# First feed-forward layer of a decoder layer: the high and low halves of the input as one moving operand of 512 columns

## The chip, the cores and the metric

The kernel runs on one core of a Trainium2 chip. The metric is the device time of one execution in microseconds (us); lower is better. The times given for a version are medians of several runs. The profile comes from one execution of its own, taken by the hardware profiler. A core has a tensor engine (PE in the profile; PEld is its loading of weights), a vector engine (DVE), a scalar engine (ACT), GpSimd (POOL), and queues that start DMA transfers (SP's is the one used most here). Tensor results land in PSUM, which has eight banks of 512 four-byte columns in each of 128 partitions; everything else works from SBUF.

## What is computed

One decoder layer on 256 positions of 2048 channels, in float32: a token mixer (three recurrent branches, far the larger part of the code) and then a gated feed-forward layer, each with a residual and a layer norm. The change touches the feed-forward part, cut here to what matters (the bias and the width-3 convolution run along the positions):

```python
def conv_ffn(h, w_up, conv_w, conv_b, w_down):       # h: (1, 256, 2048)
    hcat = causal_dwconv(h @ w_up, conv_w, conv_b)   # w_up: (2048, 2 * 5504)
    gate, up = jnp.split(hcat, 2, axis=-1)
    return (gelu(gate) * up) @ w_down                # w_down: (5504, 2048)
...
h = layer_norm(alpha * x + mix, ln1_g, ln1_b)
h = layer_norm(alpha * h + conv_ffn(h, ...), ln2_g, ln2_b)
```

## The kernel before

All large products are made from a split into two parts: a float32 operand a is rounded to float32r, the format that the matmul takes here (the high half), and the rounding's remainder is kept as a second float32r tensor (the low half). A product is then three matmuls summed in PSUM: high x high, high x low and low x high.

**Weights.** `chunks` (L216 to L243) brings a weight matrix in pieces of two contraction tiles of 128 rows (KC = 2) and up to 512 columns. A DMA on SP's queue fills `wraw` (four buffers), ScalarE casts it to `whi` (L239), VectorE subtracts to get `wlo` (L240); `whi` and `wlo` have three buffers each. These steps have high priority: the program is put in order by a scheduler that simulates the engines, and among instructions that are ready it takes those of high priority first. Each engine then runs its own list strictly in that order.

**The first layer's matmuls.** In `ffn` (L1211), the loop at L1226 goes over the 43 tiles of 128 channels two at a time, so 22 passes ("blocks", 0 to 21; the last has one tile). A block makes the gate columns and the up columns of its tiles: four column tiles of 128, two in the last block. It calls `proj_cm`, which is `cm_units` (L248): for each of the 16 contraction tiles and each column tile j, three matmuls with 128x128 weights as the stationary operand and 256 columns (the positions) of the input as the moving one:

```python
nc.tensor.matmul(a, lhsT=wh, rhs=X.h(kt), ...)   # L256: high weight, high input
nc.tensor.matmul(a, lhsT=wh, rhs=X.l(kt), ...)   # L258: high weight, low input
nc.tensor.matmul(a, lhsT=wl, rhs=X.h(kt), ...)   # L260: low weight, high input
```

Two column tiles share a PSUM bank (`acc`, pool psA, four banks), so a block takes two banks and neighbouring blocks alternate. The other four banks (pool psM: tags `mix` and `seq`, two each) belong to the mixer and to the transposes.

**What follows a block.** For each column tile, `conv` (L382) reads the bank: ScalarE makes the first tap with the bias (L384), VectorE adds two more taps, shifted by one and two positions (L387). Then Gelu on ScalarE (L1235), the product of gate and up on GpSimd (L1236), and the split into the halves of A, the second layer's input: a cast on ScalarE (L296) and a subtraction on VectorE (L297).

**The input X.** `x_pair` (L391) makes two tiles, `xh` and `xl`, of 16 contraction tiles x 256 columns each. `to_cm` (L300) fills them: it transposes the normalised rows into `mix` banks (L309), ScalarE writes the scaled high half (L314), VectorE the same in float32 (L315), and VectorE subtracts for the low half (L317). Block 0 starts while this goes on. At the same time `affine_tm` (L351) scales the rows that the residual needs, on GpSimd (L360), with the vectors of ln1 brought by DMA into the page `b4` (L358). The mixer has an X of its own from the same function.

**The second layer.** `residual_tm` (L363) runs `tm_units` (L271) with the input as the stationary operand and 512 columns of weights as the moving one (L278 to L280), two psA banks at a time, 43 contraction tiles, four times. The tile `gt`, for the ln2 vectors, takes the place of `xh` (L1239); its DMAs are issued at L1243.

Of the kernel before, what the change touches and what calls it, by code (L numbers as in the profile page):

```python
# [9 lines left out]
F32 = mybir.dt.float32  # L10
F32R = mybir.dt.float32r
AF = mybir.ActivationFunctionType
ALU = mybir.AluOpType
# [4 lines left out]
P = 128  # L18
T = 256
D = 2048  # L20
KT = D // P
KC = 2
NB = D // 512
FFN = 5504
# [154 lines left out]
class Layer:  # L179
# [68 lines left out]
    def cm_units(self, W, pieces, cts, X, nkt=KT):  # L248
# [13 lines left out]
            yield True  # L262
        return [acc[j // 2][:m, j % 2] for j, (o, m) in enumerate(cts)], acc

    def block_cm(self, W, c0, X, nct=4, nkt=KT):
        return self.proj_cm(W, [(0, c0, nct * P)], [(P * j, P) for j in range(nct)], X, nkt)

# [121 lines left out]
                                           in1=dst[:, j:], op0=ALU.mult, op1=ALU.add)  # L389

    def x_pair(self):  # L391
        return Pair([self.xp.tile([P, KT, T], F32R, name="xh")], [self.xp.tile([P, KT, T], F32R, name="xl")], KT)


    def prologue(self):
# [815 lines left out]
    def ffn(self, r):  # L1211
        nc, a, cp = self.nc, self.a, self.cp
        X = self.x_pair()
# [9 lines left out]
        where = lambda kt: (kt // 8, kt % 8) if kt < 16 else (2 + (kt - 16) // 4, kt % 4)  # L1223
        A.h = lambda kt: A.hi[where(kt)[0]][:, where(kt)[1]]
        A.l = lambda kt: A.lo[where(kt)[0]][:, where(kt)[1]]
        for c in range(0, FT, 2):  # L1226
            n = min(2, FT - c)
            ps, _ = self.proj_cm(a["ffn_w_up"], [(0, c * P, n * P), (n * P, FFN + c * P, n * P)],
                                 [(P * j, P) for j in range(2 * n)], X)
            t = [self.pg("s%d" % (i + c % 4), [P, 2, T], "fc") for i in range(2)]  # L1230
            for i in range(2):
                for j in range(n):
                    self.conv(ps[i * n + j], t[i][:, j], "fcw", 2 * FT, i * FT + c + j, 3, "fcb", fv)
            u = t[0][:, :n]
            nc.scalar.activation(out=u, in_=u, func=AF.Gelu)  # L1235
            nc.gpsimd.tensor_tensor(out=u, in0=u, in1=t[1][:, :n], op=ALU.mult)  # L1236
            i, k = where(c)
            self.split(A.hi[i][:, k:k + n], A.lo[i][:, k:k + n], u)
        gt = self.xp.tile([P, 4, 2, 512], F32, name="xh")  # L1239

        def load(j):
            for i, nm in enumerate(("ln2_g", "ln2_b")):
# [5 lines left out]
        for tt in range(2):  # L1248
            rstd, nmr, mu = self.moments(st, tt, True)
            for j in (2, 0, 1, 3):  # L1250
                t, g, b = r[j][:, tt], gt[:, j, 0], gt[:, j, 1]
# [4 lines left out]
                else:  # L1256
# [3 lines left out]
                    out=self.out[0, tt * P:(tt + 1) * P, 512 * j:512 * j + 512], in_=t)  # L1260
# [64 lines left out]
```

## Time and profile before

| | |
|---|---|
| median of 3 runs | 2454.65 us (2451.3 to 2455.12) |
| the profiled execution | 2451.87 us |
| its span, first to last instruction | 2450.1 us |
| mean granted tensor clock | 0.984 of full |
| data read, written | 430.19 MB, 14.72 MB |
| the first layer's last matmul starts | about 2202 us |

The span is what the profile's shares refer to; the rest of the execution's time lies around it. The page of a profile gives, per engine, its busy time as a share of the span, then the span in 40 slices, the DMA queues, the chain of work that ended last, and groups of instructions by source line. A group's line reads: source line, engine, operation, output tile, input tiles and shapes, count, then busy time in us and the mean duration of one in ns, then the engine's idle time just before them and what ended it. Timeline lines read: start in us, duration in us, engine, line, operation, and in brackets the idle time before it and who ended that. Matmuls are pipelined: the duration of one is longer than the distance from its start to the next one's start.

### The profile page before, as it was taken

To read this page: it belongs to the slowest core of one execution; us is meant where nothing else is said; L and a number is where in the kernel's file an instruction comes from. 1 tells how busy PE (TensorE), PEld (TensorE's weight loads), DVE (VectorE), ACT (ScalarE), POOL (GpSimd) and SP (SyncE) were. 2 spreads that over 40 slices of the span, in tenths; PEclk is the share of its full clock that TensorE was granted. 3 is DMA by queue.
4 is the path that set the end of the run, shared out by engine and by line. 5 is a ranking of instruction groups with operands and counts; after the bars stand their busy time and mean duration, and the time that the engine had idled before them with its cause. 6 is when DMAs were issued, how large, how long until landed. Compare 5 with 4: busy or idle time off the path is not lost.

```text
span 2450.1 us, 41499 instructions
## 1 busy us (share of the span) xinstructions
PE 2369.3 (97%) x16602; PEld 2131.2 (87%) x16602; DVE 1546.7 (63%) x1856; ACT 1247.3 (51%) x1648; POOL 509.5 (21%) x512
## 2 busy tenths in 40 slices
PE   7999998999999999999999998999999999999997
PEld 7898797798777899998889987787999999998886
DVE  6685575676674566786555666557766666665445
ACT  4554654556464555665434566444555455454333
POOL 0046255264363011423010001301200000000000
PEclk9899999999999999999999999999999999999999
DMA  8445454555565776665766664755655655557664
GB/s 241 144 147 164 140 158 147 154 155 164 148 186 164 213 229 179 183 190 190 263 218 188 174 181 155 238 190 175 189 182 185 185 181 182 186 169 234 194 195 148
DMA packets 283730, 447.66 MB, mean 183 GB/s; under 512 B 25816, under 2 KB 118416, under 8 KB 283152
## 3 DMA queue, kind: packets, MB, share of 16 engines
q1 hardware_dynamic: 280368, 433.99, 58.1%
q10 hardware_dynamic: 2592, 8.91, 0.9%
q8 instruction: 130, 2.13, 0.4%
q0 software_dynamic: 576, 2.10, 0.2%
q14 instruction: 64, 0.52, 0.1%
HBM read 430.19 MB, written 14.72 MB: 182 GB/s over the span
## 4 chain that ended last, share of the span: by engine, by line
PE 83%; POOL 6%; DVE 4%; ACT 3%; DMA 2%; issue 2%; SPq 0%; DVEq 0%; ACTq 0%; POOLq 0%
PE acc L256 13%; PE acc L260 13%; PE acc L258 13%; PE acc L278 13%; PE acc L279 12%; PE acc L280 12%; POOL yi L785 3%; POOL si L783 2%; POOL res L360 1%; DVE wlo L164 1%; PE mix L741 1%; ACT whi L163 1%; DVE wlo L240 1%; PE mix L628 1%; PE mix L1023 1%
## 5 line engine op out<-in xcount | busy, mean ns | idle before, releaser
L240 DVE TENSOR_TENSOR wlo<-wraw,whi 128x1024 fp32r<-128x1024 f32 (+2 forms) x548 | 703.3, 1284 | 519.5 <-ACT whi L239 514.2
L239 ACT CAST whi<-wraw 128x1024 fp32r<-128x1024 f32 (+2 forms) x548 | 569.6, 1041 | 656.5 <-PE acc L280 298.9
L256 PE MATMUL acc<-xh,whi 128*128 128x256 f32 x3104 | 885.1, 286 | 4.9 <-ACT whi L239 2.9
L260 PE MATMUL acc<-xh,wlo 128*128 128x256 f32 x3104 | 881.3, 284 | 5.0 <-DVE wlo L164 4.5
L258 PE MATMUL acc<-xl,whi 128*128 128x256 f32 x3104 | 880.9, 284 | 2.8 <-DVE xl L317 2.8
L256 PEld LDWEIGHTS acc<-xh,whi 128*128 128x128 f32 x3104 | 597.3, 193 | 9.2 <-ACT whi L239 3.5
L260 PEld LDWEIGHTS acc<-xh,wlo 128*128 128x128 f32 x3104 | 596.9, 192 | 7.9 <-DVE wlo L164 5.8
L258 PEld LDWEIGHTS acc<-xl,whi 128*128 128x128 f32 x3104 | 597.7, 193 | 4.8 <-DVE xl L317 3.7
L164 DVE TENSOR_TENSOR wlo<-wraw,whi 128x1024 fp32r<-128x1024 f32 x208 | 278.6, 1351 | 239.1 <-ACT whi L163 238.9
L163 ACT CAST whi<-wraw 128x1024 fp32r<-128x1024 f32 x208 | 216.7, 1049 | 118.3 <-PE acc L280 58.3
L279 PE MATMUL acc<-wlo,xh 128*128 128x512 f32 x640 | 255.5, 399 | 9.9 <-DVE wlo L164 9.8
L278 PE MATMUL acc<-whi,xh 128*128 128x512 f32 x640 | 262.1, 414 | 0.1
L280 PE MATMUL acc<-whi,xl 128*128 128x512 f32 x640 | 253.9, 397 | 0.0
L279 PEld LDWEIGHTS acc<-wlo,xh 128*128 128x128 f32 x640 | 122.9, 192 | 34.5 <-DVE wlo L164 12.0
L278 PEld LDWEIGHTS acc<-whi,xh 128*128 128x128 f32 x640 | 122.4, 191 | 29.5 <-issue 1.2
L280 PEld LDWEIGHTS acc<-whi,xl 128*128 128x128 f32 x640 | 122.9, 192 | 26.3
L279 PE MATMUL acc<-wlo,ah 128*128 128x512 f32 x322 | 125.4, 389 | 0.2 <-DVE wlo L240 0.2
L280 PE MATMUL acc<-whi,al 128*128 128x512 f32 x322 | 125.3, 389 | 0.0
L1236 POOL TENSOR_TENSOR fc<-fc 128x512 f32<-128x512 f32 (+1 forms) x22 | 27.9, 1268 | 453.0 <-DVE fc L387 445.0
L278 PE MATMUL acc<-whi,ah 128*128 128x512 f32 x322 | 111.9, 389 | 0.0
L785 POOL TENSOR_TENSOR yi<-yi,si 128x126 f32<-128x126 f32 (+22 forms) x124 | 84.9, 684 | 9.7
L387 DVE SCALAR_TENSOR_TENSOR fc<-acc,fcols,fc 128x255 f32<-128x255 f32 (+1 forms) x172 | 77.0, 478 | 14.0 <-ACT fc L384 12.5
(357 smaller groups left out, 3025.6 us busy)
## 6 DMA issues: line engine op xcount, KB each, us to landing
wraw<-in_w_in SPq DMA_DIRECT2D x368, 512.0 KB, 3.7
wraw<-in_ffn_w_up SPq DMA_DIRECT2D x336, 256.0 KB, 3.0
wraw<-in_ffn_w_down SPq DMA_DIRECT2D x84, 512.0 KB, 4.4
wraw<-in_proj_rwkv SPq DMA_DIRECT2D x32, 512.0 KB, 4.2
wraw<-in_proj_ssd SPq DMA_DIRECT2D x32, 512.0 KB, 4.5
wraw<-in_proj_mlstm SPq DMA_DIRECT2D x32, 512.0 KB, 4.5
wraw<-in_w_out SPq DMA_DIRECT2D x32, 512.0 KB, 4.2
gdram<-gate ACTq DMA_DIRECT2D x16, 512.0 KB, 3.4
```

Source lines behind the costliest of these rows:

```text
L163: nc.scalar.copy(out=hi, in_=self.raw[i])
L164: nc.vector.tensor_tensor(out=lo, in0=self.raw[i], in1=hi.bitcast(F32), op=ALU.subtract)
L239: nc.scalar.copy(out=hi[:, :n, :width], in_=r)
L240: nc.vector.tensor_tensor(out=lo[:, :n, :width], in0=r, in1=hi[:, :n, :width].bitcast(F32), op=ALU.subtract)
L256: nc.tensor.matmul(a, lhsT=wh[:, o:o + m], rhs=X.h(kt), start=st, stop=False, skip_group_check=True)
L258: nc.tensor.matmul(a, lhsT=wh[:, o:o + m], rhs=X.l(kt), start=False, stop=False, skip_group_check=True)
L260: nc.tensor.matmul(a, lhsT=wl[:, o:o + m], rhs=X.h(kt), start=False, stop=kt == nkt - 1, skip_group_check=True)
L278: nc.tensor.matmul(acc[tt], lhsT=X.h(kt)[:, s], rhs=wh, start=kt == 0, stop=False)
L279: nc.tensor.matmul(acc[tt], lhsT=X.h(kt)[:, s], rhs=wl, start=False, stop=False)
L280: nc.tensor.matmul(acc[tt], lhsT=X.l(kt)[:, s], rhs=wh, start=False, stop=kt == nkt - 1)
L387: nc.vector.scalar_tensor_tensor(out=dst[:, j:], in0=ps[:, :T - j], scalar=v(wname, (width - 1 - j) * nch + ct), in1=dst[:, j:], op0=ALU.m ...
L785: gps.tensor_tensor(out=Yo[:, j + 1:32, :e], in0=Yo[:, j + 1:32, :e], in1=tv, op=ALU.subtract)
```

## The change

The two halves of X become one tile, `xhl`, with the high half first; `X.both` is the whole of it. Every user of `x_pair` gets it, the mixer too; only the first feed-forward layer uses `both`. There a new function, `wide_cm`, takes the place of `proj_cm`:

- For each contraction tile and column tile, the high weight is multiplied with both halves of the input in one matmul, whose moving operand is 2 x 256 columns and whose output is a whole bank: the left half takes high x high, the right half high x low. The low weight's matmul adds to the left half.
- Each column tile so has a bank of its own, four in a block. Even blocks take them from psA, odd blocks from `mix` and `seq`.
- After the last matmul ScalarE copies each bank's right half to a scratch tile `half` in SBUF (page `b4`), and VectorE adds it onto the left half, in PSUM. The convolution then reads the left half as before.
- `gt` takes the place of the joint tile.

```diff
+    def wide_cm(self, W, pieces, n, X, odd, tmp):
+        nc = self.nc
+        acc = [self.bank(t) for t in ("mix", "mix", "seq", "seq")[:n]] if odd else [
+            self.psA.tile([P, 512], F32, name="acc") for _ in range(n)]
+        for kt, wh, wl in self.chunks(W, KT, pieces):
+            for j in range(n):
+                s = slice(P * j, P * j + P)
+                nc.tensor.matmul(acc[j].rearrange("p (a t) -> p a t", a=2), lhsT=wh[:, s], rhs=X.both[:, :, kt],
+                                 start=kt == 0, stop=False, skip_group_check=True)
+                nc.tensor.matmul(acc[j][:, :T], lhsT=wl[:, s], rhs=X.h(kt), start=False,
+                                 stop=kt == KT - 1, skip_group_check=True)
+        for j, a in enumerate(acc):
+            nc.scalar.copy(out=tmp[:, odd, j], in_=a[:, T:])
+        for j, a in enumerate(acc):
+            nc.vector.tensor_tensor(out=a[:, :T], in0=a[:, :T], in1=tmp[:, odd, j], op=ALU.add)
+        return [a[:, :T] for a in acc]
...
     def x_pair(self):
-        return Pair([self.xp.tile([P, KT, T], F32R, name="xh")], [self.xp.tile([P, KT, T], F32R, name="xl")], KT)
+        both = self.xp.tile([P, 2, KT, T], F32R, name="xhl")
+        x = Pair([both[:, 0]], [both[:, 1]], KT)
+        x.both = both
+        return x
...
+        half = self.pg("b4", [P, 2, 4, T], "half")
         for c in range(0, FT, 2):
             n = min(2, FT - c)
-            ps, _ = self.proj_cm(a["ffn_w_up"], [(0, c * P, n * P), (n * P, FFN + c * P, n * P)],
-                                 [(P * j, P) for j in range(2 * n)], X)
+            ps = self.wide_cm(a["ffn_w_up"], [(0, c * P, n * P), (n * P, FFN + c * P, n * P)], 2 * n, X,
+                              c // 2 % 2, half)
...
-        gt = self.xp.tile([P, 4, 2, 512], F32, name="xh")
+        gt = self.xp.tile([P, 2, 4, 2, 512], F32, name="xhl")[:, 0]
```

## The prediction

> **What bounds the kernel now.** I read the page first: total span, busy shares, chain of waits.
>
> ```profile
> span 2450.1 us, 41499 instructions
> PE 2369.3 (97%) x16602; PEld 2131.2 (87%) x16602; DVE 1546.7 (63%) x1856; ACT 1247.3 (51%) x1648; POOL 509.5 (21%) x512
> PE 83%; POOL 6%; DVE 4%; ACT 3%; DMA 2%; issue 2%; SPq 0%; DVEq 0%; ACTq 0%; POOLq 0%
> ```
>
> TensorE carries 83% of the chain that ended last. That is an average, so I next asked for the stage that the change touches, by windows (columns: window, its length, then PE, PEld, DVE, ACT and POOL busy with their counts, granted clock, DMA share, GB/s), and for the PE waits from 1735 us to 2260 us.
>
> ```profile
> 1690.00:1714.00 24.00, 19.22 (x132) 17.75 (x131) 20.80 (x27) 9.65 (x17) 11.26 (x4) 0.86 0.31 78
> 1714.00:1737.00 23.00, 19.80 (x157) 18.80 (x156) 21.59 (x24) 12.16 (x17) 10.29 (x4) 1.00 0.63 190
> 1867.78:1890.82 23.04, 23.04 (x194) 23.04 (x193) 14.43 (x18) 11.48 (x14) 1.29 (x1) 1.00 0.58 177
> PE acc L279 <- DVE wlo L240: 0.2, 1, 0.2
> ```
>
> Two regimes show. From block 1 on, PE never stops: one full block of the loop at L1226 is 23.04 us with PE busy in all of it, the clock granted at 1.00, and in the whole stage the only recorded PE wait is 0.2 us, after its end. VectorE has 23.04 - 14.43 = 8.61 us to spare per block, ScalarE 11.56 us. Block 0 is different: it runs while the normalised input is still being turned round, VectorE is busy 21.59 of 23 us, and PE only 19.80. So a gain in PE's own steps is worth its full size in blocks 1 to 21, and little in block 0.
>
> The third view is what one PE step takes. Busy times overlap (matmuls are pipelined), so I use starts in the timeline, not durations. First ScalarE's first convolution step of three neighbouring blocks:
>
> ```profile
> 1867.78 0.57 ACT L384 ACTIVATE fc<-acc,fcols 128x256 f32<-128x256 f32 x1 [1.24 <-PE acc L260]
> 1890.82 0.56 ACT L384 ACTIVATE fc<-acc,fcols 128x256 f32<-128x256 f32 x1 [1.24 <-PE acc L260]
> 1913.86 0.57 ACT L384 ACTIVATE fc<-acc,fcols 128x256 f32<-128x256 f32 x1 [1.24 <-PE acc L260]
> ```
>
> A block is 16 contraction tiles x 4 column tiles x 3 matmuls = 192 of 256 columns, in 23.04 us: 0.1200 us each. For 512 columns the row is the second feed-forward layer, 322 of each of its three matmuls (columns: ns min/median/max, first and last start):
>
> ```profile
> L279 PE MATMUL acc<-wlo,ah x322: 389/389/496, 2203.2 to 2421.5; 128*128 128x512 f32 x161
> 2299.78 0.39 PE L278 MATMUL acc<-whi,ah 128*128 128x512 f32 x1
> 2301.82 0.39 PE L279 MATMUL acc<-wlo,ah 128*128 128x512 f32 x1
> ```
>
> From the first to the last: 321 x 3 = 963 steps in 218.3 us, 0.2267 us; nine steps from 2299.78 to 2301.82 give 0.2267 too. The 256 extra columns cost 0.2267 - 0.1200 = 0.1067 us, and 256 columns alone would be that again: so each step of 256 carries 0.0133 us that does not grow with columns.
>
> **The change, part by part.**
>
> *Matmuls.* Per contraction tile and column tile, two steps of 256 (L256, L258) become one of 512; the third (L260) stays. 0.3600 us becomes 0.2267 + 0.1200 = 0.3467 us: 0.0133 us less. The weight load between them goes as well; PEld lies beside PE throughout, and whatever it sets is within these start-to-start times. Blocks 1 to 20 hold 64 such units each, block 21 half: 1312 units x 0.0133 = **17.5 us** gained. The trace has no 512-column operand in two runs of 256, nor a 512 step followed by a 256 step. Bounds: at best the narrow step loses its 0.0133 too, because more hides behind the wide one (35 us in all); at worst the two runs cost as two steps (0). I take 17.5, from the 512-column row, the nearest.
>
> One page speaks against a gain of this size. The Trainium skill (TensorE: Matmul & The Clock Gate, "Wait — 56ns, not 53.3ns?") puts the fixed cost of a warm back-to-back matmul at about 2.5 ns beyond its columns. By that, an estimate from that page, 1312 merged pairs would bring 3.3 us. The trace does not agree: its rows give 13.3 ns.
>
> *Evacuation.* Each column tile gets one ScalarE copy of 128x256 from PSUM and one VectorE add of 128x256 that reads and writes PSUM, 86 of each.
>
> ```profile
> L384 ACT ACTIVATE fc<-acc,fcols 128x256 f32<-128x256 f32 x86 | 46.3, 561 | 30.0 <-PE acc L260 27.9 <-DVE fc L387 2.1
> L870 ACT COPY zvo<-seq 64x256 f32<-64x256 f32 x16 | 5.9, 368 | 0.4
> L880 DVE TENSOR_TENSOR zm<-zm,seq 128x256 f32<-128x256 f32 x8 | 3.4, 419 | 5.2 <-PE seq L876 5.2
> L387 DVE SCALAR_TENSOR_TENSOR fc<-acc,fcols,fc 128x255 f32<-128x255 f32 x86 | 39.3, 478 | 12.5 <-ACT fc L384 12.5
> L315 DVE TENSOR_SCALAR tocm<-mix,cst 128x256 f32<-128x256 f32 x16 | 8.4, 539 | 2.4 <-ACT xh L314 2.4
> L297 DVE TENSOR_TENSOR al<-fc,ah 128x512 fp32r<-128x512 f32 x21 | 14.3, 680 | 0.0
> ```
>
> The copy lies between the 64-partition copy's 0.37 us and the 0.56 us of the activation that reads the same bank at the same shape; I take 0.56, the same shape. No VectorE row writes PSUM: 0.42 (a two-input add reading PSUM) to 0.54 us; I take 0.45. A full block adds 4 x 0.56 = 2.2 us to ScalarE and 4 x 0.45 = 1.8 us to VectorE: 13.7 and 16.2 us of the new 22.2 us block. Both fit, so I cost them at nothing in blocks 1 to 20. The cover is the weight pieces cut ahead, three buffers deep:
>
> ```profile
> 1877.02 1.05 ACT L239 CAST whi<-wraw 128x1024 fp32r<-128x1024 f32 x1 [0.38 <-PE acc L258]
> 1878.10 1.23 DVE L240 TENSOR_TENSOR wlo<-wraw,whi 128x1024 fp32r<-128x1024 f32 x1 [0.43 <-ACT whi L239]
> 1879.90 1.05 ACT L239 CAST whi<-wraw 128x1024 fp32r<-128x1024 f32 x1 [1.83 <-PE acc L258]
> ```
>
> A cast starts when PE lets go of the buffer, once per 2.88 us chunk, and its low half is ready at 1879.33, 2.31 us later. The piece is wanted two chunks after the release: today 5.76 - 2.31 = 3.4 us of slack, afterwards two chunks of 8 x 0.3467 = 2.77 us less 2.31, so 3.2 us. Behind a copy or a convolution step that waits stand the casts on ScalarE's queue, and behind an add the subtractions on VectorE's; as long as a cast is held up by less than 3.2 us, PE sees nothing. If that cover goes, the excess is paid at every block end.
>
> *Banks.* A block now takes four banks, even blocks the four of psA, odd blocks the mix and seq pairs. A bank is wanted again one block (22.2 us) after its block ends. VectorE's work at a block end is 4 adds, 8 taps and one split, 4 x 0.45 + 8 x 0.48 + 0.68 = 6.3 us; with 2.77 - 1.23 = 1.54 us free per chunk that takes four chunks, some 11 us. Nothing waits. The second layer takes two of psA, which block 20 held, and here the cover is only the half-length block 21:
>
> ```profile
> 2190.34 0.57 ACT L384 ACTIVATE fc<-acc,fcols 128x256 f32<-128x256 f32 x1 [1.66 <-PE acc L260]
> 2188.71 0.69 DVE L240 TENSOR_TENSOR wlo<-wraw,whi 128x512 fp32r<-128x512 f32 x1 [2.19 <-ACT whi L239]
> 2196.56 0.48 DVE L387 SCALAR_TENSOR_TENSOR fc<-acc,fcols,fc 128x254 f32<-128x254 f32 x1
> 2202.38 0.63 PE L278 MATMUL acc<-whi,ah 128*128 128x512 f32 x2
> ```
>
> Block 20 is emptied in 6.7 us (2190.34 to 2197.04), and block 21 lasts 12.0. Afterwards block 21's half-width chunks take 1.39 us and leave VectorE 1.39 - 0.69 = 0.70 us each: all four banks would take nine of them, 12.5 us, against 11.1 us (32 x 0.3467). The second layer starts with two of the four, which come first, after about half of that. I charge 0.5 us, bounds 0 to 2.
>
> *Block 0 and the joint tile.* A wide matmul needs both halves of a contraction tile, where L256 could start on the high one. The page scratch "half" takes tag b4, which GpSimd's last ln1 scaling holds:
>
> ```profile
> PE acc L258 <- DVE xl L317: 2.8, 3, 1.4
> 1720.68 0.40 PE L256 MATMUL acc<-xh,whi 128*128 128x256 f32 x2
> 1724.10 5.21 POOL L360 TENSOR_TENSOR res<-res,gb 128x1024 f32<-128x1024 f32 x2 [3.94 <-DMA gb<-in_ln_g]
> 1729.33 0.57 ACT L384 ACTIVATE fc<-acc,fcols 128x256 f32<-128x256 f32 x1 [2.82 <-PE acc L260]
> ```
>
> PE already waits for the low half, 2.8 us in three waits; before the longest of them two steps of L256 had gone ahead (1720.68), so what the wide form can lose there is two steps, 0.24 us, each time. b4 comes free at 1729.31, just as block 0 is emptied; one more scaling (half of 5.21 us) of delay would be under the 3.2 us. VectorE is full here, and four adds (1.8 us) come on top. I give block 0 no gain and a loss of 0.5 us, bounds 0 to 2. Elsewhere (the mixer's own X, the ln2 vectors that now wait for the joint tile's release instead of xh's) the same last readers stand within three matmuls, 0.36 us: nothing.
>
> *Sum.* 17.5 - 0.5 - 0.5 = 16.5 us. The profiled execution took 2451.87 us, 1.77 over its span, and lies 2.8 below the median of 2454.65: 2435.4 for it, **2438 us** against the median.
>
> **The rivals.**
>
> *The evacuation stalls PE (slower).* Place: ScalarE's queue at each block end. If the four copies and four convolution steps stand ahead of a cast, with one add between, the cast is late by 8 x 0.56 + 0.45 = 4.9 us, 1.7 us past the slack. At the ends of blocks 0 to 20 that is 21 x 1.7 = 36 us, less 17.5: 18 us slower, 2473 us. It decides from 3.2 us of delay on; at 4.1 us (0.85 past) the gain is just eaten. For it: the new add puts a VectorE turn between two ScalarE steps. Against: today's casts slip in between the convolution steps (high priority at L226), and the hold-up between two of them is 0.95 us (below); and each column tile's own bank frees the steps from each other. Chance 0.11.
>
> ```profile
> 1869.33 1.02 ACT L384 ACTIVATE fc<-acc,fcols 128x256 f32<-128x256 f32 x2
> 1871.30 1.05 ACT L239 CAST whi<-wraw 128x1024 fp32r<-128x1024 f32 x1 [0.95 <-ACT fc L384]
> ```
>
> *The step cost belongs to something that the merge keeps (no gain that can be measured).* If most of the 13.3 ns is what a weight load leaves uncovered, the two loads that remain per unit can show again what the merged step saves: the load for the next wide step has only the narrow step's 0.12 us over it. The price lies between 0 and 17.5 us of gain; I set it at a fifth, 3.5 us, less 1 for the ends: 2452 us. The page named above has a gain of nearly this size. Against: the 512-column rows carry the same 13.3 ns with 0.2267 us over each load. Chance 0.06.
>
> *Two runs cost as two steps.* The wide operand's halves lie 16 KB apart in a partition (16 x 256 elements of 4 bytes); if each run pays its own 0.0133, a unit stays at 0.36 us and the end losses remain: 2455 us. No row of that form speaks for or against. Chance 0.05.
>
> *The narrow step hides its own cost too.* 35 us less 1: 2421 us. Against: nothing shows a 256 step under 0.12 us at full clock. Chance 0.04.
>
> **How the numbers follow.** The forecast has 0.74; its own bounds are 2437 (no end loss) to 2441 us (4 us of it). For 8 in 10 the range starts lower, at 2431, for a narrow step that hides a third of its own cost too (6 us), and reaches up to the rival whose gain can't be measured, 2452; outside lie the slower case, the two runs and the full extra gain, 0.20. A difference of 0.2% is 4.9 us, about what a measurement here can tell from none. Faster by more: 0.74 + 0.04 = 0.78. Within: 0.06 + 0.05 = 0.11. Slower: 0.11.
>
> **What would show each step.** In the profile after, over a block in mid-stage: starts of a wide and the next narrow step 0.2267 and 0.1200 us apart; 1376 steps of 512 columns and as many of 256 instead of 3 x 1376; first convolution or copy steps of neighbouring blocks 22.2 us apart; no PE wait on L239 or L240 between 1735 us and the end of the stage; copies near 0.56 and adds near 0.45 us; the second layer starting some 16 us earlier, its own length unchanged. I am wrong if a unit is not near 0.347 us, if PE waits at block ends add up to more than a few us, or if the second layer's start waits for block 20's banks.

## The result and the profile after

Over four runs of each, the changed kernel takes 2437.14 us (2436.71 to 2440.01) and the kernel before 2454.89 us (2451.3 to 2455.67): a ratio of 0.9933, 95% interval 0.9921 to 0.9945, so 0.7% faster. The forecast was 2438.0 us. The profiled execution of after took 2437.14 us. Its page, answering to the three page lines of before:

```profile
span 2435.3 us, 38930 instructions
PE 2352.3 (97%) x15226; PEld 2054.2 (84%) x15226; DVE 1566.2 (64%) x1942; ACT 1274.4 (52%) x1734; POOL 512.3 (21%) x512
PE 81%; POOL 6%; DVE 5%; DMA 4%; ACT 3%; issue 2%; SPq 0%; DVEq 0%; ACTq 0%; POOLq 0%
```

There are 1376 matmuls fewer (16602 less 15226), one for each merged pair, and 86 instructions more on ScalarE (1734 against 1648) and on VectorE: the copies and the adds. The span is 14.8 us shorter. Where that lies shows in the starts. Two lines of before's PE timeline and groups (in the group: ns min/median/max, first and last start):

```profile
1690.80 0.38 PE L309 MATMUL mix<-cst,res 128*128 128x128 f32 x2
```
```profile
L278 PE MATMUL acc<-whi,ah x322: 387/389/397, 2202.4 to 2421.3; 128*128 128x512 f32 x161
```

And the same two of after:

```profile
1692.20 0.38 PE L328 MATMUL mix<-cst,res 128*128 128x128 f32 x2
```
```profile
L297 PE MATMUL acc<-whi,ah x322: 387/389/398, 2186.7 to 2406.1; 128*128 128x512 f32 x161
```

The first line is where PE turns from the mixer to the feed-forward part, 1.4 us later after the change; the second is the second layer, which starts 15.7 us earlier. So the first layer with its lead-in went from 511.6 us (2202.4 - 1690.8) to 494.5 (2186.7 - 1692.2), 17.1 us less. From the second layer's start to the end of the span it is 247.7 us before and 248.6 after. -17.1 + 1.4 + 0.9 = -14.8, the span's difference. The last two terms lie where the change moved no work, and runs of one kernel differ by more than that (above).

In the stage itself, by windows (window, length, then PE, PEld, DVE, ACT and POOL busy with counts, clock, DMA share, GB/s), first before, then after:

```profile
1800.00:1900.00 100.00, 100.00 (x836) 100.00 (x835) 64.62 (x78) 50.83 (x64) 6.46 (x5) 1.00 0.60 185
```
```profile
1714.00:1737.00 23.00, 19.95 (x111) 16.27 (x110) 22.14 (x25) 12.21 (x20) 10.22 (x4) 1.00 0.62 187
1800.00:1900.00 100.00, 100.00 (x576) 87.84 (x575) 68.54 (x97) 56.90 (x79) 6.51 (x5) 1.00 0.61 190
```

PE is full in both; the weight loads no longer are (87.84 of 100 us). ScalarE and VectorE carry 6.1 and 3.9 us more in 100 us and both are far from full. Block 0 is as the prediction found it: VectorE 22.14 of 23 us, PE 19.95. The PE waits of after between 1737 us and 2320 us have one row:

```profile
PE acc L298 <- DVE wlo L240: 0.5, 2, 0.3
```

Half a microsecond, and L298 is the second layer: no wait at any block end from block 1 on. The first copies of blocks 6 and 8 in ScalarE's timeline, one for each second block, since odd blocks use other banks:

```profile
1862.97 1.07 ACT L279 COPY half<-acc 128x256 f32<-128x256 f32 x3 [0.80 <-PE acc L276]
1907.49 1.07 ACT L279 COPY half<-acc 128x256 f32<-128x256 f32 x3 [0.80 <-PE acc L276]
```

Two blocks take 44.52 us, 22.26 each against 23.04 before. That is 44.52 / 128 = 0.3478 us for each unit of a wide and a narrow step, where 0.3467 was forecast. PE's timeline shows why it is not quite that:

```profile
1851.62 0.40 PE L274 MATMUL acc<-xhl,whi 128*128 128x512 f32 x1
...
1852.68 0.88 PE L274 MATMUL acc<-xhl,whi 128*128 128x512 f32 x3
...
1879.83 0.39 PE L274 MATMUL seq<-xhl,whi 128*128 128x512 f32 x1
1880.06 0.28 PE L276 MATMUL seq<-xhl,wlo 128*128 128x256 f32 x1
...
1882.95 0.39 PE L274 MATMUL seq<-xhl,whi 128*128 128x512 f32 x1
```

In the middle of a block nine units take 3.12 us (1879.83 to 1882.95), 0.3467 each. Shortly after the start of a block on psA, three take 1.06 us (1851.62 to 1852.68), 0.3533 each, and the wide steps show as 0.40 us instead of 0.39. PE waits in neither. So there are two rhythms, of which the prediction knew one. Within a unit of the faster one the narrow step starts 0.230 us after the wide one (1879.83 to 1880.06), and the next wide one 0.117 us after that: the sum is the forecast's, the split into 0.2267 and 0.1200 is not.

The evacuation, by groups (busy time, mean ns of one, idle before it):

```profile
L281 DVE TENSOR_TENSOR acc<-acc,half 128x256 f32<-128x256 f32 x44 | 17.0, 430 | 0.9 <-ACT half L279 0.9
L279 ACT COPY half<-acc 128x256 f32<-128x256 f32 x44 | 15.7, 375 | 11.8 <-PE acc L276 8.4 <-POOL res L379 3.4
```

A copy takes 0.375 us (0.56 was taken), an add, which reads and writes the PSUM bank itself, 0.43 (0.45).

### The profile page after: what moved, and what is told of

It reads as the page before. It is cut to its first block, busy times and chain, and to the rows that moved or that the text cites. A ratio compares the mean times of both kernels' runs of the same rounds, so it can differ in the third digit from the quotient of the medians.

```text
span 2435.3 us, 38930 instructions
## 1 busy us (share of the span) xinstructions
PE 2352.3 (97%) x15226; PEld 2054.2 (84%) x15226; DVE 1566.2 (64%) x1942; ACT 1274.4 (52%) x1734; POOL 512.3 (21%) x512
## 4 chain that ended last, share of the span: by engine, by line
PE 81%; POOL 6%; DVE 5%; DMA 4%; ACT 3%; issue 2%; SPq 0%; DVEq 0%; ACTq 0%; POOLq 0%
PE acc L297 12%; PE acc L298 12%; PE acc L299 12%; PE acc L256 7%; PE acc L260 7%; PE acc L258 7%; PE acc L274 6%; PE acc L276 3%; PE mix L274 3%; PE seq L274 3%; POOL yi L807 3%; POOL si L805 2%; PE mix L276 2%; PE seq L276 2%; DVE wlo L240 1%
## 5 line engine op out<-in xcount | busy, mean ns | idle before, releaser
L256 PE MATMUL acc<-xhl,whi 128*128 128x256 f32 x1728 | 495.4, 287 | 4.7 <-ACT whi L239 3.0
L260 PE MATMUL acc<-xhl,wlo 128*128 128x256 f32 x1728 | 491.4, 285 | 4.8 <-DVE wlo L164 4.5
L258 PE MATMUL acc<-xhl,whi 128*128 128x256 f32 x1728 | 490.6, 284 | 0.0
L256 PEld LDWEIGHTS acc<-xhl,whi 128*128 128x128 f32 x1728 | 332.8, 193 | 8.5 <-ACT whi L239 3.4
L260 PEld LDWEIGHTS acc<-xhl,wlo 128*128 128x128 f32 x1728 | 332.3, 193 | 7.6 <-DVE wlo L164 5.8
L258 PEld LDWEIGHTS acc<-xhl,whi 128*128 128x128 f32 x1728 | 333.0, 193 | 1.1 <-issue 0.7
L298 PE MATMUL acc<-wlo,xhl 128*128 128x512 f32 x640 | 254.7, 398 | 10.0 <-DVE wlo L164 9.8
L297 PE MATMUL acc<-whi,xhl 128*128 128x512 f32 x640 | 260.9, 412 | 0.1
L299 PE MATMUL acc<-whi,xhl 128*128 128x512 f32 x640 | 253.1, 396 | 0.0
L274 PE MATMUL acc<-xhl,whi 128*128 128x512 f32 x704 | 241.1, 395 | 2.1 <-DVE xhl L336 2.1
L276 PE MATMUL acc<-xhl,wlo 128*128 128x256 f32 x704 | 187.3, 281 | 0.0
L274 PEld LDWEIGHTS acc<-xhl,whi 128*128 128x128 f32 x704 | 130.2, 188 | 30.1 <-DVE xhl L336 1.3
L298 PEld LDWEIGHTS acc<-wlo,xhl 128*128 128x128 f32 x640 | 122.2, 191 | 34.6 <-DVE wlo L164 12.4
L297 PEld LDWEIGHTS acc<-whi,xhl 128*128 128x128 f32 x640 | 121.9, 190 | 29.3 <-issue 1.2
L299 PEld LDWEIGHTS acc<-whi,xhl 128*128 128x128 f32 x640 | 122.2, 191 | 26.1
L276 PEld LDWEIGHTS acc<-xhl,wlo 128*128 128x128 f32 x704 | 131.1, 190 | 3.0 <-DVE wlo L240 0.3
L274 PE MATMUL mix<-xhl,whi 128*128 128x512 f32 x352 | 125.8, 394 | 1.0 <-ACT whi L239 1.0
L298 PE MATMUL acc<-wlo,ah 128*128 128x512 f32 x322 | 125.5, 390 | 0.5 <-DVE wlo L240 0.5
```

The source lines that it names most:

```text
L256: nc.tensor.matmul(a, lhsT=wh[:, o:o + m], rhs=X.h(kt), start=st, stop=False, skip_group_check=True)
L258: nc.tensor.matmul(a, lhsT=wh[:, o:o + m], rhs=X.l(kt), start=False, stop=False, skip_group_check=True)
L260: nc.tensor.matmul(a, lhsT=wl[:, o:o + m], rhs=X.h(kt), start=False, stop=kt == nkt - 1, skip_group_check=True)
L274: nc.tensor.matmul(acc[j].rearrange("p (a t) -> p a t", a=2), lhsT=wh[:, s], rhs=X.both[:, :, kt], start=kt == 0, stop=False, skip_group_c ...
L276: nc.tensor.matmul(acc[j][:, :T], lhsT=wl[:, s], rhs=X.h(kt), start=False, stop=kt == KT - 1, skip_group_check=True)
L297: nc.tensor.matmul(acc[tt], lhsT=X.h(kt)[:, s], rhs=wh, start=kt == 0, stop=False)
```

## The experiments

All are edits of the changed kernel. Times are medians; those of the kernel before beside them are of the same chip.

**Evacuation without the merge.** Banks, copies and adds stay; the wide step is two steps of 256 again.

```diff
-                nc.tensor.matmul(acc[j].rearrange("p (a t) -> p a t", a=2), lhsT=wh[:, s], rhs=X.both[:, :, kt],
+                nc.tensor.matmul(acc[j][:, :T], lhsT=wh[:, s], rhs=X.h(kt),
                                  start=kt == 0, stop=False, skip_group_check=True)
+                nc.tensor.matmul(acc[j][:, T:], lhsT=wh[:, s], rhs=X.l(kt),
+                                 start=False, stop=False, skip_group_check=True)
```

> Banks, copies and adds as in the changed kernel, but the wide matmul is two of 256 columns again. Theory (the gain is the merged step's fixed 0.0133 us and the evacuation is hidden): 0.3600 us per unit, 46.08 us per pair of blocks, no PE waits, 2455 us as before. Rival (the gain is from one bank per column tile, or from the new order): about 2437 us. Rival (the evacuation costs PE something): over 2457 us.

Measured: 2451.66 us (2448.47 to 2455.39, ten runs) against 2453.63 before; ratio 0.9993, interval 0.9983 to 1.0002. In ScalarE's timeline the pair of blocks is back at 46.08 us, 128 x 0.3600:

```profile
1867.64 1.09 ACT L281 COPY half<-acc 128x256 f32<-128x256 f32 x3 [0.87 <-PE acc L278]
1913.72 1.10 ACT L281 COPY half<-acc 128x256 f32<-128x256 f32 x3 [0.87 <-PE acc L278]
```

So the evacuation costs nothing that can be measured, and the gain comes with the merged step; the interval leaves at most 0.2%, some 4 us, to the rest of the change.

**Merge without the evacuation.** The copies and adds are left out, and so the product of the high weights with the low half is missing from the result.

```diff
-        for j, a in enumerate(acc):
-            nc.scalar.copy(out=tmp[:, odd, j], in_=a[:, T:])
-        for j, a in enumerate(acc):
-            nc.vector.tensor_tensor(out=a[:, :T], in0=a[:, :T], in1=tmp[:, odd, j], op=ALU.add)
```

> The copies and adds are left out, so the product of high weight and low input is missing from the result; matmuls and banks as in the changed kernel. Theory (hidden): 44.52 us per pair of blocks and 2437 us, within 1 us. Rival (the evacuation costs part of the gain): less by what it costs, up to 1.4 us if it is the whole difference from the forecast unit, more if it also delays the ends of the stage.

Measured: 2439.89 us (2437.89 to 2445.66); ratio to before 0.9949, interval 0.9933 to 0.9965. Not faster than with them. ScalarE's first convolution steps (there is no copy now) of two blocks with one between:

```profile
1862.30 1.48 ACT L399 ACTIVATE fc<-acc,fcols 128x256 f32<-128x256 f32 x3 [0.80 <-PE acc L276]
1907.10 1.48 ACT L399 ACTIVATE fc<-acc,fcols 128x256 f32<-128x256 f32 x3 [0.80 <-PE acc L276]
```

44.80 us, 0.3500 a unit: the slower rhythm lasts longer here than with the copies. So the copies are not what brings it.

**One run.** The two halves of a contraction tile lie side by side, so that the wide operand is one run of 512 columns.

```diff
-        both = self.xp.tile([P, 2, KT, T], F32R, name="xhl")
-        x = Pair([both[:, 0]], [both[:, 1]], KT)
+        both = self.xp.tile([P, KT, 2, T], F32R, name="xhl")
+        x = Pair([both[:, :, 0]], [both[:, :, 1]], KT)
```

> The two halves of each contraction tile lie next to each other, so that the 512 columns are one run. In the changed kernel a pair of blocks takes 44.52 us, 0.3478 us per unit of one wide and one narrow matmul, 1.1 ns over the 0.3467 that was forecast. If the two runs cost those 1.1 ns: 44.38 us per pair of blocks, 1.4 us less in all, about 2435.7 us. If they do not (the switch between 512 and 256 columns does, or the form of the steps): 44.52 us and 2437 us. If each run of 256 paid a large part of a step's own cost, far more would come off, up to 17 us.

Measured: 2436.04 us (2433.33 to 2439.3); ratio 0.9929, interval 0.9913 to 0.9945, the same as the change's. A pair of blocks takes 44.52 us, to the hundredth that of after:

```profile
1862.52 1.07 ACT L279 COPY half<-acc 128x256 f32<-128x256 f32 x3 [0.80 <-PE acc L276]
1907.04 1.07 ACT L279 COPY half<-acc 128x256 f32<-128x256 f32 x3 [0.80 <-PE acc L276]
```

Two runs cost nothing, and the 1.1 ns by which a unit misses the forecast are not theirs.

**Copies four times.** Does ScalarE's queue hold PE up once there is more in it?

```diff
-            nc.scalar.copy(out=tmp[:, odd, j], in_=a[:, T:])
+            for _ in range(4):
+                nc.scalar.copy(out=tmp[:, odd, j], in_=a[:, T:])
```

> Each copy is made four times, 12 more per full block, 12 x 0.375 = 4.5 us more for ScalarE per block (about 17 of 22.3 us). Theory (high-priority casts slip in between the copies, so what counts is the sum per block, which still fits): no PE waits, 2437 us within 2. Rival (what stands on ScalarE's queue at a block end delays the next cast, and past 3.2 us PE pays it): (16 x 0.375 + 4 x 0.56 + 0.45) - 3.2 = 5.5 us at each of 21 block ends, about 2550 us.

Measured: 2440.30 us, one run, against 2455.66. The window:

```profile
1800.00:1900.00 100.00, 100.00 (x572) 87.10 (x571) 70.02 (x101) 70.89 (x137) 8.01 (x5) 1.00 0.60 185
```

ScalarE's share goes from 56.90 to 70.89 us, 3.1 us more in a block (copies in a row overlap, so not the expected 4.5), and PE stays full; in the whole stage there is no wait at a block end. PE has four steps fewer in the 100 us, which fits the slower rhythm and shows no stall. But the casts still get in between the copies. ScalarE's timeline, the last cast before a block's copies and the first one among them:

```profile
1861.91 1.05 ACT L239 CAST whi<-wraw 128x1024 fp32r<-128x1024 f32 x1 [1.76 <-PE acc L274]
...
1865.16 1.08 ACT L239 CAST whi<-wraw 128x1024 fp32r<-128x1024 f32 x1
```

They are 3.25 us apart, where 2.8 us is the steady distance, so a cast comes about half a microsecond late. Twelve copies more are hidden because the order keeps the casts from waiting behind them; whether PE would stall from 3.2 us of hold-up on, as the rival has it, was not reached.

**No priority.** The casts and subtractions of the first layer (block 1 on) are placed in program order, without the high priority of L226.

```diff
+                if not self.plain:
+                    nc.scalar.copy(out=hi[:, :n, :width], in_=r)
...
+            if self.plain:
                 nc.scalar.copy(out=hi[:, :n, :width], in_=r)
...
         for c in range(0, FT, 2):
+            self.plain = c > 0
```

> The first layer's casts and subtractions lose their high priority from block 0 to 21 except block 0's own; loads keep it. Theory (the priority is what keeps the cover): the copies and first taps go ahead of the casts at a block end, a cast is late by up to 4.0 us against 3.2 of slack, and PE waits about 1 us per block end, 2440 to 2460 us. Rival (three buffers cover it by themselves): 2437 us.

Measured: 2436.12 us, one run: no change. The PE waits in the same window of the trace:

```profile
PE acc L304 <- DVE wlo L242: 0.5, 2, 0.3
```

ScalarE's timeline tells why. A cast still stands between the third and the fourth copy of a block, as it does in after:

```profile
1863.03 1.05 ACT L245 CAST whi<-wraw 128x1024 fp32r<-128x1024 f32 x1
1863.98 0.38 ACT L285 COPY half<-acc 128x256 f32<-128x256 f32 x1
```

From 1737 to 2200 us ScalarE's casts, copies and convolution steps come in the same order in both traces. So the prediction's argument against the stall, that the casts slip in, is right, but the high priority is not what makes them do so in this stage. And the run that was meant to put the casts behind the copies did not: what a queue in that order would cost stays untested, as do the pieces cut ahead, which nothing here took away.

**One set of banks.** All blocks take their four banks from psA.

```diff
-        acc = [self.bank(t) for t in ("mix", "mix", "seq", "seq")[:n]] if odd else [
-            self.psA.tile([P, 512], F32, name="acc") for _ in range(n)]
+        acc = [self.psA.tile([P, 512], F32, name="acc") for _ in range(n)]
```

> Odd blocks take psA's four banks too, so every block waits for the banks of the one before. Theory (the second set hides the evacuation): PE stands at each of some 20 block ends until the first banks are emptied, 4 to 8 us each, 2520 to 2600 us. Rival (bank by bank release is enough, the other four banks are not needed): within 5 us of 2437.

Measured: 2572.88 us, one run, 135.7 over the change. PE's waits from 1737 us on (total, times, longest), then PE's timeline around one of them:

```profile
PE acc L273 <- DVE fc L405: 84.4, 20, 4.3
```
```profile
1847.89 0.63 PE L273 MATMUL acc<-xhl,whi 128*128 128x512 f32 x1 [4.31 <-DVE fc L405]
1848.31 0.41 PE L275 MATMUL acc<-xhl,wlo 128*128 128x256 f32 x1
1848.53 0.63 PE L273 MATMUL acc<-xhl,whi 128*128 128x512 f32 x1
...
1851.09 0.57 PE L273 MATMUL acc<-xhl,whi 128*128 128x512 f32 x1
```

Each block waits some 4.2 us for taps of VectorE (L405) that read the banks it needs; the eight taps of this block end at 1849.30, and PE goes on at 1847.89, so it waits for its first bank and not for all four. And then PE is slow: five units from 1847.89 to 1851.09 take 0.64 us each. The window over them (the clock is the third column from the end) shows that it is the clock:

```profile
1847.89:1851.09 3.20, 3.20 (x11) 2.71 (x12) 1.41 (x4) 0.94 (x2) 1.28 (x1) 0.52 0.29 100
```

PE was granted 0.52 of the full clock there. The slow steps cost 5 x (0.640 - 0.347) = 1.5 us more at each wait, so 84.4 + 20 x 1.5 = 114 of the 135.7 us are accounted for; the rest I did not trace. Even blocks and odd blocks on different banks are what lets the evacuation lie beside the next block.

The Trainium skill (TensorE: Matmul & The Clock Gate, "Back-to-back issue gap") has a matmul at the halved clock take its columns divided by 1.2, in ns: for this unit, as an estimate from it, 427 + 213 = 640. The rows agree, 0.42 and 0.22 us. For the full clock it has columns / 2.4 + 2.5, for the gap of a matmul by itself, without the share of its weight load. The steps here, each with a load of its own, take more: 0.2267 and 0.1200 us are 13.3 ns over the columns.

**Narrow step in two.** Is the fixed cost paid for any further step? The narrow step becomes two of 128 columns, with one weight load more.

```diff
-                nc.tensor.matmul(acc[j][:, :T], lhsT=wl[:, s], rhs=X.h(kt), start=False,
-                                 stop=kt == KT - 1, skip_group_check=True)
+                for h in range(2):
+                    nc.tensor.matmul(acc[j][:, P * h:P * h + P], lhsT=wl[:, s], rhs=X.h(kt)[:, P * h:P * h + P],
+                                     start=False, stop=kt == KT - 1, skip_group_check=True)
```

> The narrow matmul is cut into two of 128 columns with the same weights; columns and results unchanged, one step and one weight load more per unit. Theory (a fixed 0.0133 us per step beside its columns): 0.3478 + 0.0133 = 0.361 us per unit, 46.2 us per pair of blocks, 2454 us. Rival (a step can't be shorter than its weight load, which is what makes 256 columns take 0.12): 0.23 + 2 x 0.12 = 0.47 us per unit, 60 us per pair of blocks, about 2600 us.

Measured: 2577.83 us, one run, 141 over the change (2437.14). The timeline of PE and of its weight loads:

```profile
1904.68 0.45 PE L274 MATMUL acc<-xhl,whi 128*128 128x512 f32 x1
1904.96 0.33 PE L277 MATMUL acc<-xhl,wlo 128*128 128x128 f32 x2
1905.07 0.19 PEld L274 LDWEIGHTS mix<-xhl,whi 128*128 128x128 f32 x1
...
1905.18 0.42 PEld L277 LDWEIGHTS mix<-xhl,wlo 128*128 128x128 f32 x2
...
1905.59 0.45 PE L274 MATMUL mix<-xhl,whi 128*128 128x512 f32 x1
```

A unit is 0.455 us (1904.68 to 1905.59, two units): the extra step costs 0.109 us, eight times the 0.0133 of a fixed cost per step. So the prediction's sentence holds only from 256 columns up; below that something else sets the step. It fits the weight load: two loads that follow each other start 0.11 us apart (1905.07 and 1905.18), and 128 columns, at the 0.1067 / 256 us of the prediction 0.053 us, do not cover that, while 256 nearly do. This is read from the rows; no run here has a further step without its load. The Trainium skill (TensorE: Matmul & The Clock Gate, "LDWEIGHTS (loading the stationary operand)") has a load take its weight columns divided by 1.2, in ns, so 107 for 128, an estimate from it. The rows of the loads agree.

**384 and 384.** From the second contraction tile on, both steps have 384 columns of the joint tile (side by side here, too), the same sum, so that the size between is measured. For half of the tokens the product high x low is left out by it, and low x low is added to the right half for the other.

```diff
+                b = X.both[:, kt].rearrange("p a t -> p (a t)")
...
+                    nc.tensor.matmul(acc[j][:, :384], lhsT=wh[:, s], rhs=b[:, :384],
+                                     start=False, stop=False, skip_group_check=True)
+                nc.tensor.matmul(acc[j][:, :384], lhsT=wl[:, s], rhs=b[:, :384], start=False,
                                  stop=kt == KT - 1, skip_group_check=True)
```

> From the second contraction tile on both matmuls of a unit take 384 columns: the high weight leaves out the second half of the low input's columns, and the low weight adds its product with the first half of them. 768 columns and two loads per unit, as before. Theory A (columns plus 13.3 ns, a straight line from 256 to 512): 173 ns per step, 0.3467 us per unit, 44.4 us per pair of blocks, 2436 us. If the 13.3 ns at 512 are of another kind and 384 columns take their 160 ns alone: 41 us per pair, 2402 us. If changing between 512 and 256 columns is what cost the 1.1 ns over the forecast unit: 44.38 in place of 44.52 us per pair.

Measured: 2440.85 us, one run. PE's timeline:

```profile
1905.12 0.33 PE L280 MATMUL acc<-xhl,wlo 128*128 128x384 f32 x1
...
1905.64 0.33 PE L278 MATMUL acc<-xhl,whi 128*128 128x384 f32 x1
```

Three steps in 0.52 us, 0.1733 each: 384 columns at the 0.1067 / 256 us of the prediction are 0.1600, and 0.0133 is over. From 256 through 384 to 512 columns it is one straight line with one constant. This kernel is 3.7 us over the change; the first contraction tile's units, which have 512 + 384 columns here, are by the same line 82 x 0.0533 = 4.4 us longer.

**Half loads.** Does the constant go with the weights? From the second contraction tile on, only 64 of the 128 weight columns of each column tile are used, so half of the channels miss all but the first contraction tile. First with three steps of 256:

```diff
+                if kt:
+                    s = slice(P * j, P * j + 64)
+                m = s.stop - s.start
+                nc.tensor.matmul(acc[j][:m, :T], lhsT=wh[:, s], rhs=X.h(kt),
                                  start=kt == 0, stop=False, skip_group_check=True)
```

> Banks, copies and adds as in the changed kernel with three matmuls of 256 columns, as in the run with the evacuation alone, but from the second contraction tile on the weights are 64 columns wide in place of 128: half the channels get only the first contraction tile's product. The loads get shorter, the steps keep their 256 columns. Theory A (a fixed 0.0133 us per step): 120 ns per step as in the full form, 46.1 us per pair of blocks, about 2452 us. Theory B (at 256 columns the step waits for its 128-column load): between the columns' own 107 ns and 113 ns per step, 41 to 43.5 us per pair of blocks, 2400 to 2425 us.

Measured: 2424.99 us, one run. PE's timeline (128*64 are the weights):

```profile
1870.06 0.28 PE L277 MATMUL mix<-xhl,whi 128*64 128x256 f32 x1
...
1871.08 0.28 PE L277 MATMUL mix<-xhl,whi 128*64 128x256 f32 x1
```

Nine steps from 1870.06 to 1871.08 are 0.1133 us each, against 0.1200: of the 13.3 ns over the columns 6.7 are left, half, with half the weight columns. So they are no constant of a matmul. They go with the width of the weights, or with the rows of the output, which the same edit halves; the two were not tried apart.

Then the changed kernel's own wide and narrow step with the same half loads:

```diff
+                if kt:
+                    s = slice(P * j, P * j + 64)
+                m = s.stop - s.start
+                nc.tensor.matmul(acc[j][:m].rearrange("p (a t) -> p a t", a=2), lhsT=wh[:, s], rhs=X.both[:, :, kt],
                                  start=kt == 0, stop=False, skip_group_check=True)
```

> The changed kernel with weights of 64 columns from the second contraction tile on (half the channels get only the first contraction tile's product). Theory A: 0.3478 us per unit as in the changed kernel, 44.5 us per pair of blocks, 2437 us. Theory B: the narrow step falls to 107 to 113 ns and the wide one to 213 to 220, 41 to 42.6 us per pair of blocks, 2403 to 2420 us. If only the narrow one falls: 43.5 us per pair.

Measured: 2426.95 us, one run; a pair of blocks takes 43.67 us. PE's timeline:

```profile
1876.22 0.39 PE L277 MATMUL seq<-xhl,whi 128*64 128x512 f32 x1
...
1878.94 0.39 PE L277 MATMUL seq<-xhl,whi 128*64 128x512 f32 x1
```

Eight units in 2.72 us, 0.3400 each, against 0.3467: 6.7 ns less, where two steps with half of 13.3 ns each would be 13.3 ns less. Of the 26.7 ns that a unit has over its columns a quarter comes off, not half. It is no single step that keeps its cost: from wide to narrow start it is 0.228 us here (0.231 in the change), from narrow to wide 0.113 (0.117), as means over the rows from 1870 to 1890 us. Why so little comes off in this form is open.

**More blocks in the wide form.** The same form for 14 blocks of the mixer whose products take an input of the same kind, in two passes of 256 weight columns with two banks each.

```diff
+    def block_wide(self, W, c0, X, tmp):
+        for h in range(2):
+            acc = [self.psA.tile([P, 512], F32, name="acc") for _ in range(2)]
...
+                        nc.tensor.matmul(acc[j].rearrange("p (a t) -> p a t", a=2), lhsT=hi[:, k, s],
+                                         rhs=X.both[:, :, kt], start=kt == 0, stop=False, skip_group_check=True)
+                        nc.tensor.matmul(acc[j][:, :T], lhsT=lo[:, k, s], rhs=X.h(kt), start=False,
+                                         stop=kt == KT - 1, skip_group_check=True)
```

> The changed kernel, and the wide form in 14 more blocks of four column tiles, those of the mixer that are not in the hand-written order, in two passes of 256 weight columns each (two banks per pass, pieces of four contraction tiles). There PE never waits in the profile. 14 x 64 = 896 units at 0.3600 - 0.3478 = 0.0122 us: 10.9 us less, about 2426 us, 0.988 of the kernel before. Rival (two passes make the evacuation or the shorter DMA rows show, or the neighbouring work on the same engines): no gain, 2437 us or more.

Measured: 2428.26 us (2426.21 to 2430.35); ratio to before 0.9900, interval 0.9883 to 0.9916, which lies wholly under the change's. It is the fastest of all versions that compute the whole: 8.9 us under the change (7.3 when each is set against the runs of the kernel before that were made beside it), where 896 units x (0.3600 - 0.3478) = 10.9 would be all that the form can give. PE's largest waits in the mixer (300 us to 1400 us) are those of after, 6.0 and 5.7 us there:

```profile
PE acc L329 <- DVE wlo L164: 6.1, 2, 4.8
PE seq L876 <- DVE x L863: 5.7, 1, 5.7
```

**Strictly alternating.** After a block's start several wide steps stand in a row ahead of their narrow ones (the x3 in the timeline of after). Does that set the slower rhythm? The kernel of the last experiment, now with each wide step of the first layer tied behind the narrow step before it.

```diff
+        last = None
...
+                with self.tc.issue_after(last.ins) if last is not None else nullcontext():
+                    nc.tensor.matmul(acc[j].rearrange("p (a t) -> p a t", a=2), lhsT=wh[:, s], rhs=X.both[:, :, kt],
+                                     start=kt == 0, stop=False, skip_group_check=True)
+                last = nc.tensor.matmul(acc[j][:, :T], lhsT=wl[:, s], rhs=X.h(kt), start=False,
```

> The kernel with the wide form in 14 more blocks, and in the first feed-forward layer each wide matmul is kept behind the narrow one before it, so that wide and narrow alternate through the block ends too. So far some 20 of the 64 units at each second block's start run wide after wide and narrow after narrow, and units there take about 353 ns in place of 347. If that order is what costs the 1.1 ns over the forecast unit: 44.38 in place of 44.52 us per pair of blocks, and about 1.4 us less in all, 2427 us. If the grouping was what kept PE from waiting for the low weights at a block's start: PE waits on L240 appear, and a pair takes 44.6 us or more. If neither: 44.52 us.

Measured: 2431.31 us; ratio to before 0.9909, interval 0.9877 to 0.9941. The four runs are 2437.93, 2425.34, 2424.84 and 2437.27: two and two, 12 us apart. The profiled one is the first of these, and its timeline on ScalarE says:

```profile
1858.50 1.07 ACT L281 COPY half<-acc 128x256 f32<-128x256 f32 x3 [0.84 <-PE acc L278]
1903.72 1.09 ACT L281 COPY half<-acc 128x256 f32<-128x256 f32 x3 [0.83 <-PE acc L278]
```

45.22 us, 0.3533 a unit: the slower rhythm throughout, in strict alternation. So my theory that it takes the grouping has fallen. That the two faster runs ran at 0.3467 would fit their times (1312 x 0.0067 = 8.8 of the 12 us), but they have no trace. Their mean granted clock is higher too, 0.985 and 0.986 against 0.983, and for the kernel before a clock of 0.987 in place of 0.984 goes with 5 us (2448.71 and 2453.89 us, measured beside them); so the rhythm need not be all of the 12 us.

## Why the prediction was right, and where its working was not

- **The merged step** (17.5 us of gain) was right in its place and nearly in its size. Splitting it again takes the gain away. Measured by the unit it is 1312 x (0.3600 - 0.3478) = 16.0 us; 1.5 us are lost to the slower rhythm, which no row of before showed.
- **"Each step of 256 carries 0.0133 us that does not grow with columns"** is right as a number from 256 to 512 columns, as long as all steps have one size, and too wide as a reason. Where wide and narrow steps take turns only the sum of two holds (0.230 + 0.117). With half the weight columns half of it goes from steps of 256, but a quarter from a wide and a narrow one. And a further step of 128 columns costs 0.109 us. At the halved clock it is not there at all (0.64 us a unit). The forecast came out because the change keeps 128 weight columns, at least 256 moving columns and the full clock. What the cost is made of stays open.
- **The evacuation** at nothing in blocks 1 to 20 was right: the changed kernel has no wait at a block end, and four copies in place of one do not bring one. Of the reasons, that the casts slip in between was right, and that the priority makes them was wrong: without it ScalarE keeps the same order. The slack of 3.2 us was never used up, so no run says whether it is the right bound. The copy was taken at 0.56 us, by the row of the same shape, and is 0.375 us, beside the 64-partition copy that was the lower bound.
- **The banks** were right. With one set PE waits 84.4 us.
- **The ends** were mis-sized, in sign too: 1.0 us of loss was charged for block 0 and the second layer's start. The first layer with its lead-in gained 17.1 us, the units 16.0 of it, so by these two traces 1.1 us were gained there. It is not shown that the wide form gained them. In block 0 of after, while the last quarter of the input is still being turned round, four wide steps of block 1 go ahead (two on `mix`, two on `seq`, 0.9 us of work). But in the run without the merge, steps of block 1 go ahead there too, with a wait of the same length behind them. First after, then that run:

```profile
1725.36 0.73 PE L274 MATMUL mix<-xhl,whi 128*128 128x512 f32 x2 [0.97 <-ACT whi L239]
...
1727.43 0.50 PE L274 MATMUL acc<-xhl,whi 128*128 128x512 f32 x1 [0.88 <-DVE xhl L336]
```
```profile
1725.78 0.30 PE L274 MATMUL mix<-xhl,whi 128*128 128x256 f32 x1
...
1727.69 0.39 PE L276 MATMUL acc<-xhl,whi 128*128 128x256 f32 x1 [0.90 <-DVE xhl L338]
```

And counted from where PE turns to the feed-forward part, ScalarE begins to empty block 1 after 61.8 us in before, 59.3 in after, and 59.6 in the run without the merge. So most of what was gained by then comes without the merged step. Which part of the rest of the change brings it, no run says.

- **The page "half"** gave the coincidence that the prediction named. ScalarE's timeline of after shows block 0's copies waiting for GpSimd's scaling to let the page go, and at the end of that block PE waited 0.24 us in all, and for a low half of the weights, not for the page:

```profile
1729.66 0.92 ACT L279 COPY half<-acc 128x256 f32<-128x256 f32 x3 [3.40 <-POOL res L379]
```

- **The rivals.** The stall did not come, not even with the copies made four times, though its condition, a cast held up by more than 3.2 us, was not reached there either. The cost of two runs is ruled out by the one run. The narrow step that hides its own cost did not come. "The step cost belongs to something that the merge keeps" may be half right in its mechanism, since the cost changes with the width of the weights or the output, and was wrong in its price: of the 17.5 us that the merged steps were to save, 16.0 were saved.
- **The sum** against the profiled execution was 16.5 us and the span shows 14.8, split under the result above. Against the medians it is 17.75, because before's profiled execution, 2451.87 us, was one of its short ones. That the median came within 0.9 us of the forecast is luck in part: the merged step was taken 1.5 us too high and the ends 2.1 us too low (a loss of 1.0 for a gain of 1.1), and runs of one kernel lie up to 4 us apart.

## What to carry to other kernels

Before you count a step's fixed cost as saved, ask what it goes with: here it shrinks with the width of the weights (or of the output), and each step brings a weight load, so it is not simply a price per step. Two products that share a weight tile are worth one step of 512 columns, while cutting a step under 256 costs eight times what a merge brings. A result that has to be collected afterwards was free here, where the next block has banks of its own; without them the same copies and taps cost 136 us, some 30 of it by slow steps after the waits. Look at the order in the trace before you conclude from a run that was meant to change it. And a reason that leads to the right number (the constant per step, the priority) still has to be tried, or it will be carried to a kernel where it fails.

## What the runs showed of the hardware that was not expected

- The same alternating pair of a 512-column and a 256-column matmul runs at 0.3467 us or at 0.3533 us, at the full granted clock, without a wait that the profile shows. The slower one is there with the input as one run, without the copies, and in strict alternation, so it needs neither two runs, nor copies, nor wide steps in a row. What decides between them is open.
- A further step of 128 columns, with a weight load of its own, costs 0.109 us, where 128 columns more in an existing step cost 0.053 (half of 0.1067).
- After a wait of 4.3 us PE ran at half the clock for 3.2 us (0.52 granted), and in such steps the 13.3 ns are missing: 768 columns take 0.640 us, twice 768 times the 0.1067 / 256 us. The kernel before has such steps too, at the start of block 0 (its PE timeline; the clock granted from 1698.45 to 1699.09 is 0.50): three take 0.64 us, the same as a wide and a narrow one at that clock. By these rows a merge saves nothing there.

```profile
1698.45 0.41 PE L260 MATMUL acc<-xh,wlo 128*128 128x256 f32 x1
...
1699.09 0.41 PE L260 MATMUL acc<-xh,wlo 128*128 128x256 f32 x1
```
